# Adding expert rows into the residual in DRAM, and a planned order for the tail

## The chip, the core and the metric

One core of one Trainium2 chip runs the whole kernel. The metric is device microseconds of one launch. The engines are TensorE (PE; PEld is its weight load), VectorE (DVE), ScalarE (ACT), GpSimd (POOL) and SyncE (SP), which only issues transfers here.

## The reference, cut to what matters

One layer of a residual block over 1024 tokens of width 1024. The mixers and the router lie ahead of the change. What follows them is this:

```python
hf = _rmsnorm(x, g_ffn[i]).reshape(B * S, D)
eid, gate = _hier_route(hf, w_group[i], b_group[i], w_expert[i], b_expert[i])
x = x + _routed_experts(hf, eid, gate, w1[i], w3[i], w2[i]).reshape(B, S, D)
e = _rmsnorm(p[i] @ w_ple[i], g_ple_proj[i])
pg = jax.nn.sigmoid(_rmsnorm(x, g_ple[i]) @ w_ple_gate[i])
x = x + pg * e
return _rmsnorm(x, g_final)
```

`_rmsnorm(x, g)` is `x * rsqrt(mean(x*x) + EPS) * g`. Each token goes to 2 of 32 experts of hidden width 512; an expert computes `(silu(xb @ w1) * (xb @ w3)) @ w2`, times the token's gate. `p` has 256 columns.

## The kernel before, in words

Tokens lie in 8 tiles of 128. Products in full precision are made of three matmuls: each operand is split into a high part (`split_hi`, a ScalarE copy, L235) and a low part (`split_lo`, L238, a subtraction on VectorE or GpSimd), and high by high, high by low and low by high are summed in PSUM (`mmr`, L244).

The first stage (mixers, output projection, router) is written as generators whose steps a planner, `Flow` (L63), puts in an order: `go` is an operation with an assumed duration, `get` and `put` count buffers, `on` and `mark` are dependences, `fork` starts another generator. Rank decides between operations that could start within 0.25 us of each other, the lower first. The order in which the planner releases the generators is the order of the instructions on each engine's queue; each engine runs its queue in that order. `c_mix` stores the residual after the mixers to `x2_d` and its norm to `hf_d`, both in DRAM. `c_route` and `tables` (L1099) sum, with one-hot matmuls into `stab`, four columns per expert and slot: the token, the destination row, and two parts of the gate. `fill` (L943) builds their right-hand sides.

The expert loop (L1538) goes over 192 units; an expert has four units for `w1` and `w3` (`up`) and two for `w2` (`down`), and the units of neighbouring experts are interleaved. A unit's two tiles of 512 KB are loaded 13 units ahead (`AHEAD`) and split 2 units ahead (`SL`). Tokens are gathered from `hf_d` by GpSimd (`gather`, L1348), transposed and split. `out_rows` (L1524) scales an expert's output by the gate (`ys`) and scatters its rows (`scatter`, L1353) to `y_d`, which has a row for each token and choice; consecutive scatters are declared independent. The last expert's SiLU, transposes and split (`act_T`) run one behind the other ahead of its `down` units.

The tail is in an order written out by hand (L1567 to L1705). `p` (tiles 4 to 7) and `w_ple` are split, `ple(i)` makes `p @ w_ple` for tiles 5 to 7 in PSUM, squares it for the norm and multiplies by `gp`; tiles 0 to 4 were made in the first stage and are loaded from `e_d` (`e_load`). The gate weights are loaded (`load_wg`, three of them after `last_ys`, three after the first load of `y_d`) and split, five of eight on GpSimd (`WGP`). For each tile `post_load` reads `x2_d`, `load_y` reads the two rows of each token from `y_d` and waits for all scatters, `post_norm` adds them (L1630), squares, and multiplies by the norm factor and `gpl` (L1637) before the transposes; `post_mm` makes the gate product `pg`, 48 matmuls of 512 columns a tile; `post_out` applies the sigmoid, multiplies, adds, norms and stores. The last tile's product is made in two halves of 512 columns.

## Time and profile before

| | us |
|---|---|
| median of 3 runs | 1086.72 (1086.24 to 1089.61) |
| profiled execution, its own time | 1087.43 |
| span of its trace, first to last instruction | 1085.7 |
| mean granted TensorE clock | 0.984 |

The busy time of an engine is the time in which its instructions ran; a matmul's row lasts longer than the step to the next one, since matmuls are pipelined. The granted clock is a share of full speed: 1.00 is 2.4 GHz, 0.50 is 1.2 GHz. The share of the transfers is the mean over 16 transfer engines; where packets overlap it goes above 1. "Idle before" names what ended an engine's wait.

### The profile page before, as it was taken

How to read it: one execution, taken by the hardware profiler on the slowest of the kernel's cores; microseconds unless marked ns; L12 is line 12 of the kernel's file. 1: busy time of each engine (PE TensorE's matmuls, PEld its weight loads, DVE VectorE, ACT ScalarE, POOL GpSimd, SP SyncE). 2: the span in 40 equal slices, each digit the busy share in tenths (PEclk: the TensorE clock that was granted, in tenths of full speed). 3: DMA queues.
4: the chain of work that ended last, by engine and by line, in shares of the span. 5: the costliest groups of instructions: out<-in, count | busy, mean ns of one | idle time of the engine just before them, and what ended most of it. 6: DMA issues, size and time to landing. Idle time of an engine off the chain costs nothing. (4 is left out here: it accounts for less than half of the span.)

```text
span 1085.7 us, 14177 instructions
## 1 busy us (share of the span) xinstructions
PE 1021.4 (94%) x4839; PEld 838.6 (77%) x4840; DVE 931.0 (86%) x1109; ACT 727.3 (67%) x932; POOL 281.9 (26%) x235
## 2 busy tenths in 40 slices
PE   4999999979999799999999999999999999867995
PEld 4887768758888688888888888888888888655884
DVE  5999999999556699999999999999999999669863
ACT  5447878772333688888888888888787888643331
POOL 6459576631210210111111111111010100033110
PEclk9999999999999899999999999999999999979998
DMA  9310002243326889999999999999999999477511
GB/s 270 99 39 20 19 20 78 96 155 118 117 97 207 311 315 405 400 403 401 381 395 391 381 402 385 388 392 385 382 385 382 385 379 394 154 275 290 174 40 58
DMA packets 101070, 281.49 MB, mean 259 GB/s; under 512 B 16849, under 2 KB 34945, under 8 KB 100993
## 3 DMA queue, kind: packets, MB, share of 16 engines
q1 hardware_dynamic: 89216, 255.79, 63.2%
q0 software_dynamic: 10592, 21.01, 5.2%
q10 hardware_dynamic: 1184, 3.75, 0.9%
q8 instruction: 39, 0.64, 0.2%
q14 instruction: 39, 0.31, 0.1%
HBM read 265.28 MB, written 31.98 MB: 274 GB/s over the span
## 5 line engine op out<-in xcount | busy, mean ns | idle before, releaser
L1349 POOL DMA_INDIRECT xg<-hf_d,toki x32 | 43.8, 1370 | 361.0 <-PE xgT L295 348.6
L549 DVE SCALAR_TENSOR_TENSOR fir<-u,V,fir 128x512 f32<-128x512 f32 (+20 forms) x180 | 133.2, 743 | 5.0
L235 ACT ACTIVATE xTh<-xgT 128x512 fp32r<-128x512 f32 x80 | 47.1, 598 | 77.3 <-PE xgT L295 77.3
L584 POOL TENSOR_TENSOR acc<-fpr,acc 128x512 f32<-128x512 f32 x60 | 86.2, 1437 | 40.6 <-ACT fpr L574 37.6
L1354 POOL DMA_INDIRECT y_d<-ys,dsti x32 | 39.1, 1220 | 147.9 <-ACT ys L1526 147.9
L287 POOL TENSOR_TENSOR rs<-ms,mhalf 128x1 f32<-128x1 f32 x32 | 23.2, 727 | 155.2 <-DVE ms L281 155.2
L238 DVE TENSOR_TENSOR xTl<-xgT,xTh 128x512 fp32r<-128x512 f32 x80 | 54.4, 686 | 6.8 <-ACT xTh L235 6.8
L244 PE MATMUL zvg<-hTh,whi 128*128 128x512 f32 (+1 forms) x144 | 56.7, 394 | 0.0
L244 PE MATMUL zvg<-hTh,wlo 128*128 128x512 f32 (+1 forms) x144 | 53.2, 369 | 0.0
L244 PE MATMUL zvg<-hTl,whi 128*128 128x512 f32 (+1 forms) x144 | 53.0, 368 | 0.0
L574 ACT ACTIVATE fpr<-u,V 128x512 f32<-128x512 f32 x60 | 41.9, 717 | 15.4 <-POOL acc L584 15.3
L295 PE MATMUL xgT<-ident,xg 128*128 128x128 f32 x256 | 38.8, 276 | 7.0 <-DVEq L1423 7.0
L295 PEld LDWEIGHTS xgT<-ident,xg 128*128 128x128 f32 x256 | 32.2, 142 | 14.9 <-issue 7.1
L1526 ACT ACTIVATE ys<-ey,gat 128x1024 f32<-128x1024 f32 x32 | 35.4, 1107 | 7.1 <-PE ey L244 7.1
L244 PE MATMUL wo<-wohi,lnyhl 128*128 128x512 f32 x128 | 39.4, 404 | 0.7 <-DVE lnyhl L238 0.7
L238 POOL TENSOR_TENSOR wlo<-wraw,whi 128x1024 fp32r<-128x1024 f32 x14 | 34.3, 2453 | 20.2 <-ACT whi L235 20.2
L1383 ACT ACTIVATE silu<-eab 128x512 f32<-128x512 f32 x32 | 19.2, 599 | 29.0 <-PE eab L244 29.0
L855 ACT ACTIVATE hf<-xre 128x1024 f32<-128x1024 f32 x8 | 8.5, 1058 | 42.0 <-DVE xre L843 33.4
L244 PE MATMUL pg<-wglo,xTh 128*128 128x512 f32 x96 | 32.0, 401 | 3.6 <-POOL wglo L238 2.3
L244 PE MATMUL pg<-wghi,xTl 128*128 128x512 f32 x96 | 31.7, 398 | 1.5 <-DVE xTl L238 1.5
L244 PE MATMUL pg<-wghi,xTh 128*128 128x512 f32 x96 | 32.4, 404 | 0.2 <-ACT xTh L235 0.2
L244 PEld LDWEIGHTS zvg<-hTl,whi 128*128 128x128 f32 x144 | 27.7, 192 | 5.8 <-issue 1.7
(3324 smaller groups left out, 3514.3 us busy)
## 6 DMA issues: line engine op xcount, KB each, us to landing
wraw<-in_w_in_dram SPq DMA_DIRECT2D x16, 512.0 KB, 5.1
yy<-y_d SPq DMA_DIRECT2D x16, 512.0 KB, 5.1
xin<-in_x_dram SPq DMA_DIRECT2D x8, 512.0 KB, 7.1
woraw<-in_w_out_dram SPq DMA_DIRECT2D x8, 512.0 KB, 3.7
xre<-in_x_dram SPq DMA_DIRECT2D x8, 512.0 KB, 4.1
hf_d<-hf POOLq DMA_DIRECT2D x8, 512.0 KB, 5.2
x2r<-x_d SPq DMA_DIRECT2D x8, 512.0 KB, 8.0
wgraw<-in_w_ple_gate_dram SPq DMA_DIRECT2D x8, 512.0 KB, 6.1
```

The lines of the kernel that those rows point to most:

```text
L235: act.activation(r_(hi), src, AF.Copy)
L238: (eng or dve).tensor_tensor(out=r_(lo), in0=src, in1=hi, op=ALU.subtract)
L244: pe.matmul(out=o, lhsT=r_(l), rhs=r_(r), start=start, stop=stop)
L287: pool.tensor_tensor(out=rs, in0=ms, in1=mhalf[:, 0:1], op=ALU.pow)
L295: pe.transpose(out=t[:, k * P:(k + 1) * P], in_=src[:, off + k * P:off + (k + 1) * P], identity=ident)
L549: dve.scalar_tensor_tensor(f[:, a0 - t0:512], u[c][:, a0 - s:t1 - s], tap(c, s), f[:, a0 - t0:512], op0=ALU.mult, op1=ALU.add)
L574: act.activation(pr, u[c][:, 512 - s:1024 - s], AF.Copy, scale=tap(c, s))
L584: pool.tensor_tensor(out=a[:, 512:1024], in0=fprs.pop((c, s)), in1=a[:, 512:1024], op=ALU.add)
L1349: return pool.indirect_dma_start(out=dst, out_offset=None, in_=hf_d, in_offset=bass.IndirectOffsetOnAxis(ap=idx, axis=0), bounds_check=S - ...
L1354: return pool.indirect_dma_start(out=y_d, out_offset=bass.IndirectOffsetOnAxis(ap=idx, axis=0), in_=src, in_offset=None, bounds_check=2 * ...
L1383: act.activation(s_, w[:, 0:512], AF.Silu)
L1526: i = act.activation(ys, yw.pop(e), AF.Copy, scale=gat[:, e:e + 1])
```

## The change

- `scatter` adds the rows of an expert to `x2_d` in the transfer itself (`compute_op`), with the token as the row. `y_d`, the destination column of the tables and the declared independence of the scatters go.
- The tail reads `x2_d` alone. `g_ple` is multiplied into `w_ple_gate` where that is split (`c_wg`), all low parts on VectorE. The raw residual is transposed; its norm factor is the scale of the sigmoid.
- The loads and splits of `p` and `w_ple` and the loads of the gate weights come into the expert loop (`past` counts the units since the last weight load).
- The last two units and the whole tail are ordered by a second planner run. The last expert's output is scaled in two halves, one on ScalarE and one on VectorE. The first tile of `x2_d` is loaded in two halves. The last gate product is made in cuts of 512, 256 and 256 columns, and the last tile is scaled and stored in two halves by two engines.

```diff
+             ("lru_b_r", 4), ("lru_b_i", 4), ("lru_lambda", 4), ("lru_conv_w", 16), ("g_ffn", 8), ("g_ple", 8)]
...
-    gv = [cst.tile([P, NT, 4], F32, name="gv%d" % k) for k in range(2)]
+    gv = [cst.tile([P, NT, 3], F32, name="gv%d" % k) for k in range(2)]
     for k in range(2):
-        for t in range(2):
-            pool.iota(gv[k][:, :, t], pattern=[[P, 8]], base=1 + S * k * t, channel_multiplier=1,
-                      allow_small_or_imprecise_dtypes=True)
+        pool.iota(gv[k][:, :, 0], pattern=[[P, 8]], base=1, channel_multiplier=1, allow_small_or_imprecise_dtypes=True)
...
         dve.tensor_scalar(tok, T[:, 0:NE], -1.0, None, op0=ALU.add)
-        dve.tensor_scalar(dst, T[:, NE:2 * NE], -1.0, None, op0=ALU.add)
-        dve.tensor_copy(gat, T[:, 2 * NE:3 * NE])
-        dve.tensor_tensor(out=gat, in0=gat, in1=T[:, 3 * NE:4 * NE], op=ALU.add)
+        dve.tensor_copy(gat, T[:, NE:2 * NE])
+        dve.tensor_tensor(out=gat, in0=gat, in1=T[:, 2 * NE:3 * NE], op=ALU.add)
 
...
     def scatter(src, idx):
-        return pool.indirect_dma_start(out=y_d, out_offset=bass.IndirectOffsetOnAxis(ap=idx, axis=0),
-                                       in_=src, in_offset=None, bounds_check=2 * S - 1, oob_is_err=False)
+        return pool.indirect_dma_start(out=x2_d, out_offset=bass.IndirectOffsetOnAxis(ap=idx, axis=0),
+                                       in_=src, in_offset=None, bounds_check=S - 1, oob_is_err=False,
+                                       compute_op=ALU.add)
 
...
     def out_rows(e):
         ys = m4("ys")
-        i = act.activation(ys, yw.pop(e), AF.Copy, scale=gat[:, e:e + 1])
-        sc = scatter(ys, dsti[:, e:e + 1])
-        if scs:
-            tc.declare_no_dep(sc.ins, scs[-1].ins, reason="every row has one writer")
-        scs.append(sc)
-        return i
+        act.activation(ys, yw.pop(e), AF.Copy, scale=gat[:, e:e + 1])
+        scatter(ys, toki[:, e:e + 1])
+
+    wgr = {}
+    pl = {}, {}, {}
+
+    def load_wg(k):
+        wgr[k] = slot("wgraw")
+        load(wgr[k], A["w_ple_gate"][0][rows(k), :])
 
...
+    for s, (e, g) in enumerate(units[:-2]):
+        past = s + AHEAD - len(units)
+        if past == 0:
+            pt = p_load(1)
+        elif past == 1:
+            pw = {k: wp_load(k) for k in range(2)}
+        elif past > 2 and len(wgr) < 8:
+            load_wg(len(wgr))
+        load_unit(s + AHEAD)
...
+        if past in (5, 6):
+            k = past - 5
...
+            pl[0][1, k], pl[1][1, k] = o[:, 0:512], o[:, 512:1024]
+        elif past in (7, 8):
+            k = past - 7
+            hi, lo = slot("wphi"), slot("wplo")
+            split_hi(hi, pw[k])
+            split_lo(lo, pw[k], hi)
+            pl[2][k] = hi, lo
+    fl = Flow({"s": NSLOT - 24, "m4": NM, "m2": 4, "wp": 1, "yp": 1, "tp": 2, "a": 4}, OFF2)
+    fl.table = "silu"
...
+    def c_last():
+        e = NE - 1
+        yield get("m2")
+        yield go("ACT", 0.75, set="silu")
+        w = abw.pop(e)
+        s_ = m2("silu")
+        act.activation(s_, w[:, 0:512], AF.Silu)
+        yield go("DVE", 0.69)
+        dve.tensor_tensor(out=s_, in0=w[:, 512:1024], in1=s_, op=ALU.mult)
+        yield put("wp")
+        yield get("tp")
+        yield go("PE", 0.45, lag=0.35)
+        t = act_tr(s_)
+        yield put("m2")
+        yield get("m2", 2)
+        hi, lo = m2("hhi"), m2("hlo")
+        yield go("ACT", 0.6)
+        split_hi(hi, t)
+        yield go("DVE", 0.69)
+        split_lo(lo, t, hi)
+        yield put("tp")
+        yield get("yp")
+        w = None
+        for j in range(4):
+            yield go("PE", 6 * MM, lag=0.35 if j == 3 else 0.0)
+            w = w or ytile()
+            y_mm(w, (hi, lo), j, his[len(units) - 2 + j // 2][j % 2])
+            if j == 3:
+                yield put("m2", 2)
+            yield put("s", 2)
+        yield get("m4")
+        ys = m4("ys")
+        yield ("fork", -90, c_half(w, ys))
+        yield go("ACT", 0.6)
+        act.activation(ys[:, 0:512], w[:, 0:512], AF.Copy, scale=gat[:, e:e + 1])
+        yield on("ys1")
+        yield put("yp")
+        yield go("POOL", 1.1, lag=4.5)
+        scatter(ys, toki[:, e:e + 1])
+        yield put("m4")
+        yield mark("sc")
+
+    def c_half(w, ys):
+        yield go("DVE", 0.69)
+        dve.tensor_scalar(ys[:, 512:1024], w[:, 512:1024], gat[:, NE - 1:NE], None, op0=ALU.mult)
+        yield mark("ys1")
+
...
+    def c_ple2(i):
+        yield get("wp")
+        w = None
+        for k in range(2):
+            for si in range(3):
+                yield go("PE", 2 * MM, lag=0.35 if k and si == 2 else 0.0)
+                w = w or wtile("ple")
+                ple_mm(w, i, pl, [(k, si)])
+        yield get("s")
+        es_[i] = slot("er")
+        yield ("fork", -1, c_esq(i, w))
+        yield on("gp")
+        yield go("DVE", 1.22)
+        dve.tensor_tensor(out=es_[i], in0=w, in1=gpb, op=ALU.mult)
+        yield on(("eq", i))
+        yield put("wp")
+        yield mark(("e", i))
+
...
+    def c_wg(k):
+        yield get("s", 2)
+        yield go("ACT", 1.05)
         hi, lo = slot("wghi"), slot("wglo")
...
+        act.activation(r_(hi), wgr[k], AF.Copy, scale=vec("g_ple", k))
+        yield go("DVE", 1.22, port=True)
+        dve.scalar_tensor_tensor(r_(lo), wgr[k], vec("g_ple", k), hi, op0=ALU.mult, op1=ALU.subtract)
+        yield put("s")
+        wgs[k] = (hi, lo)
+        yield mark(("wg", k))
+
+    def c_x2(i):
+        yield on("sc")
+        if i >= 2:
+            yield on(("xT", i - 2, 1))
+        yield get("s")
         xs[i] = slot("x2r")
...
+        if i == 0:
+            yield ("fork", -59.5, c_xh())
+        yield go("SP", 0.7 if i == 0 else 1.35, lag=2.6)
+        cs = slice(0, 512 if i == 0 else D)
+        load(xs[i][:, cs], x2_d[rows(i), cs])
+        yield mark(("xl", i))
+        if i == 0:
+            yield on("xh")
+        yield mark(("x", i))
+
+    def c_xh():
+        yield go("SP", 0.7, lag=2.6)
+        load(xs[0][:, 512:D], x2_d[rows(0), 512:D])
+        yield mark("xh")
+
+    def c_xt(i):
+        yield on(("xl", i))
+        if i:
+            yield on(("xt", i - 1))
+        yield get("a", 2)
+        xT[i] = aslot("xTh"), aslot("xTl")
+        for q in range(2):
+            yield on(("x" if q else "xl", i))
+            yield get("tp")
+            yield go("PE", 0.45, lag=0.35)
+            t = ttile("x2T")
+            transposes(t, xs[i], off=q * 512)
+            yield ("fork", -40, c_xs(i, q, t))
+        yield mark(("xt", i))
+
+    def c_xs(i, q, t):
+        qs = slice(q * 512, (q + 1) * 512)
+        yield go("ACT", 0.6)
+        split_hi(xT[i][0][:, qs], t)
+        yield go("DVE", 0.69)
+        split_lo(xT[i][1][:, qs], t, xT[i][0][:, qs])
+        yield put("tp")
+        yield mark(("xT", i, q))
+
...
+    def c_pg(i, n):
+        last = i == NT - 1
+        cuts = ((0, 512), (512, 768), (768, 1024)) if last else ((0, 1024),)
+        if i:
+            yield on(("pgd", i - 1))
+        yield get(psum(n))
+        w = None
+        ss = sm("ss5", 3) if last else sm("ss5")
+        for c, (a, b) in enumerate(cuts):
             for k in range(8):
...
+                yield on(("xT", i, k // 4))
+                yield on(("wg", k))
+                yield go("PE", 6 * MM * (b - a) / 1024, lag=0.35 if k == 7 else 0.0)
+                w = w or ptile(n)
+                hi, lo = wgs[k]
                 ks = slice(k * P, (k + 1) * P)
...
+                xh, xl = xT[i]
+                for si, (l_, rr) in enumerate(((xh[:, ks], hi), (xh[:, ks], lo), (xl[:, ks], hi))):
+                    for o in range(a, b, 512):
+                        e = min(o + 512, b)
+                        mmr(w[:, o:e], l_, rr[:, o:e], k == 0 and si == 0, k == 7 and si == 2)
+            if c == len(cuts) - 1:
+                yield mark(("pgd", i))
+                yield put("a", 2)
+            yield ("fork", 20 + i, c_out(i, n, c, len(cuts), a, b, w, ss))
+
+    def c_out(i, n, c, nc_, a, b, w, ss):
+        f = (b - a) / 1024
+        cs = slice(a, b)
+        yield on(("rsx", i))
+        yield on(("e", i))
+        if c == 0:
+            yield get("m4")
+            sgs[i] = m4("sgp")
+        sg, xt, e = sgs[i], xs[i], es_[i]
+        yield go("ACT", 0.17 + 0.9 * f, set="sig")
+        act.activation(sg[:, cs], w[:, cs], AF.Sigmoid, scale=rsx[:, i:i + 1])
+        if c == nc_ - 1:
+            yield put(psum(n))
+        yield go("DVE", 0.14 + 1.08 * f, port=True)
+        dve.scalar_tensor_tensor(sg[:, cs], sg[:, cs], rse[:, i:i + 1], e[:, cs], op0=ALU.mult, op1=ALU.mult)
+        yield go("DVE", 0.14 + 1.08 * f, port=True)
+        dve.tensor_tensor(out=xt[:, cs], in0=xt[:, cs], in1=sg[:, cs], op=ALU.add)
+        yield go("ACT", 0.36 + 0.9 * f)
+        act.activation(sg[:, cs], xt[:, cs], AF.Square, accum_out=ss[:, c:c + 1])
+        yield mark(("sq", i, c))
+        if nc_ > 1:
+            yield on("gfin")
+            yield go("DVE", 0.14 + 1.08 * f, port=True)
+            dve.tensor_tensor(out=xt[:, cs], in0=xt[:, cs], in1=gfin[:, cs], op=ALU.mult)
+            yield mark(("xf", c))
+        if c < nc_ - 1:
+            return
+        for k in range(nc_):
+            yield on(("sq", i, k))
+        yield put("s")
+        yield put("m4")
+        if nc_ > 1:
+            yield go("DVE", 0.2)
+            s1 = sm("ss6")
+            dve.tensor_reduce(s1, ss, op=ALU.add, axis=AX.X)
+            ss = s1
+        yield go("DVE", 0.15)
+        ms = ms_of(ss, D)
+        yield go("POOL", 0.55)
+        rs = rs_of(ms)
+        if nc_ > 1:
+            yield ("fork", -1, c_end(xt, rs))
+            yield go("DVE", 0.4)
+            dve.tensor_scalar(xt[:, 512:D], xt[:, 512:D], rs, None, op0=ALU.mult)
+            yield go("SP", 0.7, lag=2.6)
+            load(out[0][rows(i), 512:D], xt[:, 512:D])
+            return
+        yield on("gfin")
+        yield go("DVE", 1.22, port=True)
+        dve.scalar_tensor_tensor(xt, xt, rs, gfin, op0=ALU.mult, op1=ALU.mult)
+        yield go("SP", 1.35, lag=2.6)
+        load(out[0][rows(i), :], xt)
+        yield put("s")
+
+    def c_end(xt, rs):
+        yield go("ACT", 0.6)
+        act.activation(xt[:, 0:512], xt[:, 0:512], AF.Copy, scale=rs)
+        act.dma_start(out=out[0][rows(NT - 1), 0:512], in_=xt[:, 0:512])
+
+    fl.add(-90, c_last())
+    fl.add(-99, c_vec(gpb, A["g_ple_proj"], "gp"))
+    for k in range(8):
+        fl.add(RK2["wg"] + k, c_wg(k))
+    for i in range(NPG):
+        fl.add(RK2["e"] + i, c_e(i))
     for i in range(NPG, NT):
...
+        fl.add(RK2["ple"] + i, c_ple2(i))
+    fl.add(-10, c_vec(gfin, A["g_final"].unsqueeze(0), "gfin"))
     for i in range(NT):
...
+        fl.add(-60 + i, c_x2(i))
+        fl.add(-50 + i, c_xt(i))
+        fl.add(RK2["xrs"] + i, c_xrs(i))
+        fl.add(10 + i, c_pg(i, i))
+    fl.add(0, c_free([("e", i) for i in range(NPG, NT)], 6))
+    fl.run()
+    mctx.close()
```

## Rows read from the trace of the kernel before

**Rows 1.** The page, busy time: us, share of the span, instructions.

```profile
PE 1021.4 (94%) x4839; PEld 838.6 (77%) x4840; DVE 931.0 (86%) x1109; ACT 727.3 (67%) x932; POOL 281.9 (26%) x235
```

**Rows 2.** Busy us and instructions by stretch; then granted clock, transfers' share, GB/s.

```profile
500.00:700.00 200.00, 200.00 (x948) 165.28 (x947) 185.38 (x181) 164.25 (x191) 28.82 (x22) 1.00 1.01 390
...
923.00:939.00 16.00, 16.00 (x73) 12.93 (x71) 14.76 (x14) 12.83 (x14) 0.97 (x1) 1.00 0.51 190
...
948.00:960.00 12.00, 9.81 (x36) 7.84 (x36) 3.37 (x5) 4.51 (x7) 1.05 (x2) 0.86 0.63 223
960.00:968.00 8.00, 0.26 (x2) 0.00 (x0) 6.04 (x9) 4.12 (x8) 1.59 (x3) 0.82 1.02 407
968.00:975.00 7.00, 5.72 (x16) 4.24 (x17) 7.00 (x5) 5.59 (x7) 6.75 (x4) 0.50 0.60 229
975.00:993.00 18.00, 12.42 (x53) 8.77 (x51) 15.91 (x14) 7.06 (x10) 11.20 (x5) 0.99 0.73 283
993.00:1074.00 81.00, 80.59 (x380) 67.21 (x380) 57.97 (x67) 27.45 (x46) 9.54 (x13) 1.00 0.33 119
...
988.00:994.00 6.00, 2.85 (x15) 2.03 (x16) 6.00 (x9) 4.54 (x6) 1.40 (x1) 1.00 1.03 419
```

**Rows 3.** The chain that ended last: start us, us, what.

```profile
972.85 2.72 DVE x2r L1630
...
979.31 4.57 DMA x2r<-x_d
...
999.61 0.88 PE xgT L295 x8
...
1055.56 18.84 PE pg L244 x83
```

**Rows 4.** Groups by line and shape, 945 to 1086: busy us, mean ns.

```profile
L1630 DVE TENSOR_TENSOR x2r<-x2r,yy 128x1024 f32<-128x1024 f32 x16 | 22.7, 1416 | 0.1
...
L238 POOL TENSOR_TENSOR wglo<-wgraw,wghi 128x1024 fp32r<-128x1024 f32 x5 | 14.7, 2968 | 0.1
```

**Rows 5.** Timeline of TensorE, 938 to 1000: start us, us, instruction.

```profile
940.45 0.66 PE L295 MATMUL hTp<-ident,silu 128*128 128x128 f32 x4 [1.41 <-DVE silu L1384]
...
946.92 0.62 PE L244 MATMUL ey<-ehi__9264,hlo 128*128 128x512 f32 x2
...
959.64 0.61 PE L244 MATMUL ple<-wphi,phl 128*128 128x512 f32 x2
968.02 1.97 PE L295 MATMUL xgT<-ident,n 128*128 128x128 f32 x8 [7.76 <-DVE ms L281]
```

**Rows 6.** Timeline of all engines around the last scatter.

```profile
948.98 0.97 POOL L1354 DMA_INDIRECT y_d<-ys,dsti  x1 [12.98 <-ACT ys L1526]
...
956.26 0.80 SPq L1622 DMA_DIRECT2D yy<-y_d  x2
```

**Rows 7.** Timeline of ScalarE at the start.

```profile
4.40 1.06 ACT L311 ACTIVATE xn<-xin 128x1024 f32<-128x1024 f32 x1 [0.96 <-DMA xin<-in_x_dram]
```

**Rows 8.** The tile ys: ns min/median/max, first and last start us.

```profile
L1526 ACT ACTIVATE ys<-ey,gat x32: 1102/1107/1121, 402.1 to 947.6; 128x1024 f32<-128x1024 f32 x32
L1354 POOL DMA_INDIRECT y_d<-ys,dsti x32: 972/1239/1247, 403.5 to 949.0; - x32
...
DMA to landing us min/median/max: 7.0/7.6/8.7
```

**Rows 9.** The tile sgp: ns min/median/max, by shape at the end.

```profile
L1664 DVE SCALAR_TENSOR_TENSOR sgp<-sgp,rse,er x9: 746/1276/1286, 995.1 to 1075.1; 128x1024 f32<-128x1024 f32 x7, 128x512 f32<-128x512 f32 x2
```

**Rows 10.** The output in DRAM: issue to landing of its nine stores.

```profile
DMA to landing us min/median/max: 2.0/2.6/3.1
```

**Rows 11.** Timeline of TensorE, two matmuls of 256 columns in sequence.

```profile
24.43 0.28 PE L244 MATMUL zvg<-hTl,whi 128*128 128x256 f32 x1
24.55 0.28 PE L244 MATMUL zvg<-hTh,wlo 128*128 128x256 f32 x1
```

**Rows 12.** Timeline of VectorE at the end of the kernel.

```profile
1078.39 1.41 DVE L1672 SCALAR_TENSOR_TENSOR x2r<-x2r,rs,gfin 128x512 f32<-128x512 f32 x2 [0.73 <-POOL rs L287]
```

More of the change, by code (lines that the diff above doesn't have):

```diff
@@ L35 @@
 NA = 5
-GM = 1
 HS = 5
@@ L39 @@
 EARLY = (3, 4, 5, 6, 7, 8, 9)
-PN0 = 6
 NPG = 5
-WGP = (1, 2, 3, 4, 5)
-PLU = 0
-PLW = 0
-WG0 = 2
-WG1 = 5
+OFF2 = {}
+RK2 = {"pT": -30, "wp": -29, "wg": 0, "e": 12, "ple": -5, "xrs": 2}
 WDVE = (8, 11)
@@ new lines, in _body @@
+    rsx = cst.tile([P, NT], F32, name="rsx")
+    def c_last():
[39 more added lines that the diff above has]
+        yield mark("sc")
@@ L1615, in post_load @@
-    def post_load(i):
-        xs[i] = slot("x2r")
-        load(xs[i], x2_d[rows(i), :])
-    def load_y(i):
-        for k in range(2):
-            yys[i, k] = m4("yy")
-            q = nc.sync.dma_start(out=yys[i, k], in_=y_d[k * S + i * P:k * S + (i + 1) * P, :])
-            for sc in scs:
-                order(q, sc, True)
-        return q
-    def post_norm(i):
-        xt = xs[i]
-        for k in range(2):
-            a = dve.tensor_tensor(out=xt, in0=xt, in1=yys.pop((i, k)), op=ALU.add)
-            if k == 0:
-                order(a, ei[PN0 if i == 0 else NT - 1])
-        ss = sm("ss4")
-        n3 = m4("n3")
-        act.activation(n3, xt, AF.Square, accum_out=ss)
-        rs = rstd_of(ss, D)
-        dve.scalar_tensor_tensor(n3, xt, rs, gpl, op0=ALU.mult, op1=ALU.mult)
-        xTp[i] = gather_T(n3)
@@ L1675, in _body @@
-    post_load(0)
-    for k in range(WG0):
-        load_wg(k)
-    load(gpl, A["g_ple"].broadcast_to([P, D]))
-    for k in range(WG0, WG1):
-        order(load_wg(k), last_ys, True)
-    y0 = load_y(0)
-    for k in range(WG1, 8):
-        order(load_wg(k), y0)
-    post_load(1)
-    load_y(1)
-    gfin = slot("gfin")
-    load(gfin, A["g_final"].unsqueeze(0).broadcast_to([P, D]))
-    for i in range(NPG, NT):
-        ple(i)
-        if i == PN0:
-            post_norm(0)
-    for i in range(8):
-        split_wg(i)
```

205 lines of the change are left out of this document (79 added, 126 removed).

## The prediction

> **What bounds the kernel now.** I began with the page. TensorE is busy 1021.4 of 1085.7 us [rows 1], so a gain has to come from its gaps or from the work after its last matmul. The busy time by stage says where the gaps are [rows 2]. While the experts run, from 500 to 700, TensorE is busy 200 of 200 us, VectorE 185.4, ScalarE 164.3, and the transfers move 390 GB/s. From 993 to 1074 TensorE is full again, and nothing else is near its limit. Between them lies the poor stretch: 9.8 of 12 us busy from 948 to 960, 0.3 of 8 to 968, 5.7 of 7 to 975 at a granted clock of 0.50 (the 1.2 GHz level), 12.4 of 18 to 993. That is 16.8 us without a matmul, and more than 3 us of half speed.
>
> The chain of waits names what stands there [rows 3]: adding the two expert rows to the residual on VectorE (L1630, 2.72 us in one piece of the chain), a reload of the residual (4.57 us), transposes. The groups of this stretch by shape give the volume [rows 4]: 16 adds of 22.7 us in all, and five splits of the gate weights on GpSimd that take 14.7 us, 2.97 each. So the tail waits behind four things in a row: the last scatter, reading both expert rows back, adding and normalising on VectorE, and splitting weights late.
>
> The last scatter and the work around it are in the timeline [rows 5, 6]. The last expert's output matmuls end at about 947.4, its scatter is issued at 948.98, and the first read of its rows at 956.26, when it has landed: 7.3 us. TensorE ends the three `ple` products at about 960.2 (959.64 and one piece) and transposes nothing until 968.02.
>
> **The change part by part.** I follow one chain, from the last expert to the end, on the clock of the profiled execution (1087.43 us, span 1085.7).
>
> *Start and routing.* One small load more on ScalarE's queue (`g_ple`): an issue takes 0.40 us on SP (two in 0.80 [rows 6]), and ScalarE waits 0.96 us for `x` there [rows 7], which hides it. `fill` writes 96 columns a tile instead of 128 and `tables` has one operation less. I take -0.3 us for these; between -0.5 and +0.5.
>
> *Scatter with add, experts 0 to 30.* Experts are 17.6 us apart (31 steps from 402.1 to 947.6), a scatter lands in 7.6 us [rows 8]. Consecutive scatters now wait for each other, since the declaration that they are independent is gone; that wait ends some 10 us before the next one is issued, and the gathers queued behind it on GpSimd lose nothing. What is not seen in this trace is an adding transfer. Below, it costs nothing beyond a plain one. Nearest above: it reads the destination too. An expert has 2048/32 = 64 rows of 4 KB, 0.262 MB; at 419 GB/s, the rate of the stretch from 988 to 994, in which the transfers never stood [rows 2], that is 0.63 us per expert. The stage moves 390 GB/s where 419 are to be had, so the transfers have 17.6 x (1 - 390/419) = 1.2 us to spare per expert. Cost taken: 0. The cover is this 1.2 us; if it is gone, every microsecond above it costs 31.
>
> A rule bears on this: the Trainium skill, "Collectives: The Full Stack", section "The bandwidth ceiling", holds that an add in the transfer engine costs no cycles of its own but a second source read, on the same ring as the first. By it the adding scatter takes the 0.63 us above and the stage stays TensorE's; no run so far shows it here.
>
> *Work moved into the expert loop.* Two groups of four transposes of `p`, with their splits, and the split of `w_ple` come into units 184 to 187. TensorE gets eight transposes, 0.88 us at full clock [rows 3]: +0.9. VectorE gets two splits of 512 and two of 1024 columns, some 3.6 us, where it has 14.8 of 16 us busy from 923 to 939 [rows 2], 1.2 us free. Splits run two units (near 6 us) ahead of their matmuls, so the rest is taken from that lead; cost 0, at most 2.
>
> *Last expert.* Its SiLU, transposes and split leave TensorE a hole (1.41 us of it before the transposes [rows 5]) which the plan fills with `ple` pieces of 0.45 us. The planner counts the low part's split before it releases the output matmuls, so I expect about three pieces too many in front of them: +1.4 (0 to 2). Scaling the output as two halves on two engines takes 0.75 us (the half pass of [rows 9]) for 1.11 [rows 8] and saves 0.4. The scatter is issued at 948.98 - 0.3 + 0.9 + 1.4 - 0.4 = 950.6.
>
> *Its landing.* 7.3 us for the plain one. Lower end: no difference. Upper end: a second trip as long as the first, 14.6. The data of one scatter are little and the way is mostly latency, so I stay near the plain row and add 1.5 us for reading first: 959.4.
>
> *To the first gate matmul.* No rows to add, no norm: the half tile of `x2_d` is issued (0.3) and lands (2.6 us, the median of the output stores [rows 10]; 2.0 to 4.6, the reload in the chain [rows 3]). Four transposes at the low clock take 1.0 (eight took 1.97 [rows 5]); ScalarE's high half 0.6. First gate matmul: 963.9. By then the gate weights are split: their loads are issued from unit 182 on, and ScalarE and VectorE have over 20 us from the end of the expert loop for eight passes each of at most 1.28 us [rows 9]. The five GpSimd splits become VectorE's; the cover is the wait for the scatter, and without it they would cost up to 6 us.
>
> *Gate products.* 360 matmuls of 512 columns at 0.227 us, the pitch of the last piece of the chain (83 in 18.84 us [rows 3]), 81.6 us; the last half tile in two cuts of 256, 48 at 0.12 [rows 11], 5.8; 60 transposes left at 0.11 (eight in 0.88 [rows 3]), 6.6. TensorE will have idled from about 954 to 962; before, after an idle of 7.8 us, it worked 7 us at the 0.50 clock [rows 2, 5]. I charge the same: half of 7.4, 3.7. Sum 97.7, end at 1061.6. A tile takes TensorE 48 x 0.227 + 8 x 0.11 = 11.8 us; VectorE needs two half passes and four whole ones for it, 6.6 us by [rows 9], ScalarE no more, and the `x2` and `e` loads of 0.5 MB each come where the transfers run at a third of their rate [rows 2]. So the plan has room. The norm factor as the sigmoid's scale and `g_ple` in the weights take a VectorE pass of 1.28 us per tile out of the path into TensorE; that is how the 963.9 comes about, and is not counted again.
>
> *End.* The last matmul ends at 1074.4 [rows 3], 0.2 us after its slot; from the slot to the end of the span there are 11.5 us. Four steps shrink from 512 to 256 columns: 0.746 against 1.276 us for twice the width [rows 9] gives about 0.25 each, 1.0. The two closing multiplications, 1.41 us one behind the other [rows 12], run side by side in 0.7. One small reduction stays as it was. 11.5 - 1.6 = 9.9 us: 1071.5.
>
> The span falls by 14.2 us, the profiled 1087.43 to 1073.2. The median of the runs, 1086.72, stands 0.7 lower, so **1072.5 us**.
>
> **The rivals.**
> *The transfers become the bound (slower).* If an adding row costs much more than one extra read, the expert stage goes to the speed of the transfers. Price: per expert, what the adds cost beyond 1.2 us, 31 times. The gain of 14.2 us is gone at 0.46 us beyond, 1.7 us of extra transfer time per scatter, 2.7 plain reads of its rows. At four reads, 2.5 us, it is 31 x 1.3 = 40 us: 1112.8 us. For it: 390 of 419 GB/s is close. Against: 1.7 us is much for 0.262 MB that a plain transfer moves in 0.63. Chance 0.10.
>
> *The wait is only moved.* The adding scatter lands in 14.6 us, and with nothing left for TensorE to do the whole 5.8 us more show: 1078.3. For it: the landing is mostly fixed latency, and a read before the write may double it. Chance 0.13.
>
> *The planned tail starves TensorE.* Order on four in-order queues is fixed from estimated times; if a slot or an engine is late by 1.8 us for each of eight tiles, the gain is gone: 1087. Against: VectorE at half load, ScalarE below. Chance 0.06.
>
> *Better than forecast.* The hole holds just the pieces that fit, the add costs no landing time, the clock stays up: 1.4 + 1.5 + 3.7 less, 1065.9. Against: the same idle of 8 us did lower the clock. Chance 0.11.
>
> *It does not do what it says*: some wait for the whole residual in DRAM could hold the first loads back until much later than the last scatter; that has the look and the price of the third rival and is counted there.
>
> **How the numbers follow.** 0.60 is left for the forecast. Its own terms reach from -5 (no added landing, no surplus pieces, and half the clock's charge) to +7 (2 us of late splits, 3 us of stalls in the tail, 2 us of slower loading). The range takes in the good case and the moved wait: 1065 to 1081, leaving out the first and third rivals and a little of the rest. A measurement can tell 0.3%, 3.3 us, from no change. Faster by more: forecast, moved wait, better case, 0.84, of which 0.01 is taken off for a tail that loses part of its gain: 0.83. Slower by more: the first rival (0.10) and a sliver of the third, 0.11. Between: 0.06.
>
> **What would show it.** Right: expert spacing still 17.6 us and TensorE still 200 of 200 from 500 to 700, at some 400 GB/s; the last scatter issued near 950.6 and read from near 959.4; the first gate matmul near 964, and TensorE without gaps from about 970 to 1062; under 10 us after it. Wrong: TensorE waiting for expert weights and a spacing above 17.8 us; a last scatter of over 11 us; idle TensorE between gate tiles; an unlowered clock near 965.

## The result, and the profile after

The changed kernel is **slower**: 1115.99 us in the median of 4 runs (1114.17 to 1117.82) against 1087.26 us for the kernel before, ratio 1.026, 95% interval 1.024 to 1.028. I had forecast 1072.5, so 43.5 us are to be explained.

The page of the changed kernel, its busy time and the head of its chain of waits:

```profile
span 1116.1 us, 14187 instructions
...
PE 1034.1 (93%) x4863; PEld 840.4 (75%) x4864; DVE 901.2 (81%) x1094; ACT 740.4 (66%) x936; POOL 295.5 (26%) x228
...
DMA 37%; PE 26%; DVE 3%; ACT 2%; issue 2%; SPq 0%; POOLq 0%; ACTq 0%; DVEq 0%
```

TensorE has the same work as before [rows 1], but the chain that ended last now runs over transfers for 37% of the span. The stretches say where (columns as in [rows 2]):

```profile
500.00:700.00 200.00, 194.42 (x900) 155.85 (x899) 176.22 (x173) 161.46 (x184) 35.34 (x21) 1.00 0.99 366
700.00:900.00 200.00, 194.74 (x898) 155.60 (x897) 174.09 (x171) 159.72 (x182) 36.73 (x21) 1.00 0.99 364
940.00:960.00 20.00, 10.10 (x47) 8.16 (x45) 10.39 (x10) 8.67 (x10) 1.59 (x1) 0.84 1.00 374
...
994.00:1000.00 6.00, 1.65 (x8) 1.03 (x6) 4.96 (x6) 1.32 (x4) 4.39 (x3) 0.83 0.20 27
1000.00:1010.00 10.00, 5.16 (x17) 4.00 (x18) 3.15 (x5) 2.83 (x5) 0.00 (x0) 0.50 0.85 307
1010.00:1074.00 64.00, 64.00 (x301) 52.97 (x300) 29.66 (x41) 24.09 (x38) 6.80 (x11) 0.99 0.26 92
```

From 500 to 700 TensorE does 900 matmuls where it did 948 [rows 2], and the transfers, busy throughout, move 366 GB/s and not 390: the expert stage has become theirs. ScalarE's splits wait here for loads of weights, up to 2.7 us at a time; in the kernel before they never did from 500 to 900. (The 366 counts no second read by the add: the profile has 256.37 MB read from HBM here and in e9_free below, which leaves the add out. Counted once per expert, 0.262 MB would make it 380.) Ahead of the tail, from 940 to 960, TensorE works 10.1 of 20 us. From 1010 on it is full, as forecast. The tile `ys` of the changed kernel (ns min/median/max, first and last start):

```profile
L1343 POOL DMA_INDIRECT x_d<-ys,toki x32: 1574/1962/5932, 404.6 to 994.3; - x32
L1512 ACT ACTIVATE ys<-ey,gat x31: 1096/1102/1112, 403.2 to 976.6; 128x1024 f32<-128x1024 f32 x31
...
DMA to landing us min/median/max: 5.9/9.3/11.0
```

The first `ys` comes 1.1 us later than before, and the scatter lands in 9.3 us and not 7.6 [rows 8]. The last of these 31 stands behind a wait that happens once, shown below; so I take the spacing from the second expert to the thirtieth, 28 steps, in every run. The same tile in that stretch, kernel before and changed kernel:

```profile
L1526 ACT ACTIVATE ys<-ey,gat x29: 1102/1107/1112, 419.8 to 917.4; 128x1024 f32<-128x1024 f32 x29
```

```profile
L1512 ACT ACTIVATE ys<-ey,gat x29: 1096/1102/1112, 420.9 to 942.4; 128x1024 f32<-128x1024 f32 x29
```

The experts lie (942.4 - 420.9)/28 = 18.62 us apart, where before it was 17.77. The timeline of TensorE (waits in brackets) has the second loss and the tail:

```profile
949.50 0.60 PE L288 MATMUL hTp<-ident,silu 128*128 128x128 f32 x4
964.32 1.09 PE L1158 MATMUL pT<-ident,p_in 128*128 128x128 f32 x4 [14.21 <-DMA p_in<-in_p_dram]
...
983.19 0.66 PE L288 MATMUL hTp<-ident,silu 128*128 128x128 f32 x4 [0.99 <-DVE silu L1586]
...
986.88 0.62 PE L238 MATMUL ey<-ehi__9265,hhi 128*128 128x512 f32 x2
...
1002.88 1.12 PE L288 MATMUL x2T<-ident,x2r 128*128 128x128 f32 x4 [7.23 <-DMA x2r<-x_d]
...
1007.07 1.09 PE L288 MATMUL x2T<-ident,x2r 128*128 128x128 f32 x4 [1.79 <-DMA x2r<-x_d]
1007.80 1.20 PE L238 MATMUL pg<-wghi,xTh 128*128 128x512 f32 x2
```

TensorE's queue stood 14.2 us at the transposes of `p`, with ready matmuls of the last two experts behind them. Why the load was late is in the timeline of SP:

```profile
949.03 0.33 SPq L235 DMA_DIRECT2D eraw__8956<-in_w_dram  x1
952.70 0.33 SPq L235 DMA_DIRECT2D eraw__8958<-in_w_dram  x1
953.95 0.39 SPq L235 DMA_DIRECT2D p_in<-in_p_dram  x1
```

`p_in` stands behind all expert weights in SP's queue, which the transfers now hold back. From the last scatter, at 994.27, to the end take 121.8 us, where before it was 1085.7 - 948.98 = 136.7 and my forecast had 1071.5 - 950.6 = 120.9. The tail gained nearly what it should; the last scatter goes out 45.3 us later than before and 43.7 later than forecast.

### The profile page after: what moved, and what is told of

It reads as the page before. It is cut to its first block, busy times and chain, and to the rows that moved or that the text cites. A ratio compares the mean times of both kernels' runs of the same rounds, so it can differ in the third digit from the quotient of the medians.

```text
span 1116.1 us, 14187 instructions
## 1 busy us (share of the span) xinstructions
PE 1034.1 (93%) x4863; PEld 840.4 (75%) x4864; DVE 901.2 (81%) x1094; ACT 740.4 (66%) x936; POOL 295.5 (26%) x228
## 3 DMA queue, kind: packets, MB, share of 16 engines
HBM read 256.37 MB, written 31.98 MB: 258 GB/s over the span
## 4 chain that ended last, share of the span: by engine, by line
DMA 37%; PE 26%; DVE 3%; ACT 2%; issue 2%; SPq 0%; POOLq 0%; ACTq 0%; DVEq 0%
PE ey L238 8%; PE eab L238 7%; PE pg L238 6%; PE ple L238 2%; DMA eraw__4845<-in_w_dram 1%; DMA eraw__7573<-in_w_dram 1%; DMA eraw__8121<-in_w_dram 1%; DMA eraw__4152<-in_w_dram 1%; DMA eraw__6176<-in_w_dram 1%; DMA eraw__5630<-in_w_dram 1%; DMA eraw__4538<-in_w_dram 1%; DMA eraw__8360<-in_w_dram 1%; DMA eraw__7450<-in_w_dram 1%; DMA eraw__6722<-in_w_dram 1%; DMA eraw__4661<-in_w_dram 1%
## 5 line engine op out<-in xcount | busy, mean ns | idle before, releaser
L1338 POOL DMA_INDIRECT xg<-hf_d,toki x32 | 48.7, 1521 | 352.2 <-PE xgT L288 339.8
L1343 POOL DMA_INDIRECT x_d<-ys,toki x32 | 64.8, 2026 | 168.6 <-ACT ys L1512 161.2
L229 ACT ACTIVATE xTh<-xgT 128x512 fp32r<-128x512 f32 x64 | 37.6, 589 | 13.6 <-PE xgT L288 13.0
L232 DVE TENSOR_TENSOR xTl<-xgT,xTh 128x512 fp32r<-128x512 f32 x64 | 43.6, 684 | 0.5 <-ACT xTh L229 0.5
L1790 DVE SCALAR_TENSOR_TENSOR sgp<-sgp,rse,er 128x1024 f32<-128x1024 f32 (+2 forms) x10 | 10.7, 1071 | 37.0 <-ACT sgp L1786 37.0
L280 POOL TENSOR_TENSOR rs<-ms,mhalf 128x1 f32<-128x1 f32 x24 | 14.2, 593 | 93.9 <-DVE ms L274 93.8
L238 PE MATMUL pg<-wghi,xTh 128*128 128x512 f32 (+1 forms) x104 | 34.1, 391 | 1.4 <-ACT sgp L1786 1.4
L1512 ACT ACTIVATE ys<-ey,gat 128x1024 f32<-128x1024 f32 x31 | 34.2, 1102 | 0.0
L238 PE MATMUL pg<-wglo,xTh 128*128 128x512 f32 (+1 forms) x104 | 32.8, 378 | 0.0
L238 PE MATMUL pg<-wghi,xTl 128*128 128x512 f32 (+1 forms) x104 | 32.8, 378 | 0.0
```

The lines of the kernel that those rows point to most:

```text
L229: act.activation(r_(hi), src, AF.Copy)
L232: (eng or dve).tensor_tensor(out=r_(lo), in0=src, in1=hi, op=ALU.subtract)
L238: pe.matmul(out=o, lhsT=r_(l), rhs=r_(r), start=start, stop=stop)
L280: pool.tensor_tensor(out=rs, in0=ms, in1=mhalf[:, 0:1], op=ALU.pow)
L1338: return pool.indirect_dma_start(out=dst, out_offset=None, in_=hf_d, in_offset=bass.IndirectOffsetOnAxis(ap=idx, axis=0), bounds_check=S - ...
L1343: return pool.indirect_dma_start(out=x2_d, out_offset=bass.IndirectOffsetOnAxis(ap=idx, axis=0), in_=src, in_offset=None, bounds_check=S - ...
```

## The experiments

**1. The changed kernel without the add, and with `p` later.** The first leaves the add out (rows overwrite); the second moves two steps by three and two units.

```diff
 e1_plain
-            in_=src, in_offset=None, bounds_check=S - 1, oob_is_err=False,
-            compute_op=ALU.add)
+            in_=src, in_offset=None, bounds_check=S - 1, oob_is_err=False)
 e2_later
-        if past in (5, 6):
+        if past in (8, 9):
-        elif past in (7, 8):
+        if past in (9, 10):
```

> The changed kernel with plain scatters into the residual, the add left out (so the expert rows replace the residual rows instead of being added); every wait between scatters stays. Theory A (the second read of an adding transfer costs the expert stage): spacing of the experts from 500 to 900 back from 18.9 to 17.7 us, transfers back to some 390 GB/s, time near 1080 to 1090. Rival C (the scatters' waits for each other, or the residual as destination, cost the time): spacing stays at 18.9, time stays near 1116.

> The changed kernel with the transposes of p three units later and the splits of w_ple two units later in the expert loop. Theory (TensorE's queue stood 14.2 us behind a transpose of p whose load had not landed): the wait is gone, time near 1102, and the expert spacing stays at 18.9. Rival (the last experts' weights would have been late by as much): under 4 us gained, 1112 or more.

Measured: 1082.65 us and 1107.96 us, one run each. The tile `ys` of e1_plain, then of e2_later, from the second expert to the thirtieth:

```profile
L1511 ACT ACTIVATE ys<-ey,gat x29: 1103/1105/1115, 421.4 to 918.7; 128x1024 f32<-128x1024 f32 x29
```

```profile
L1512 ACT ACTIVATE ys<-ey,gat x29: 1095/1100/1112, 420.2 to 939.4; 128x1024 f32<-128x1024 f32 x29
```

Without the add the spacing is (918.7 - 421.4)/28 = 17.76 us, that of the kernel before, although the scatters still wait for each other and go to the residual: rival C falls. With the add it is 18.54. e2_later made the wait at `p` shorter and did not end it:

```profile
961.24 1.12 PE L1158 MATMUL pT<-ident,p_in 128*128 128x128 f32 x4 [5.72 <-DMA p_in<-in_p_dram]
```

So its theory (no wait, near 1102) and its rival (under 4 us gained) both missed. There are two losses, and the add is the larger: 33.3 us between the changed kernel and e1_plain, against 8.0 for moving `p`.

**2. Are the scatter's rows dealt unevenly to the transfer engines?** The slots of an expert were spread over all partitions; e4_both has the later `p` as well.

```diff
+    pool.iota(slots.rearrange("p (a b) -> p a b", a=16), pattern=[[1, 16], [16, 8]], base=0,
+              channel_multiplier=0, allow_small_or_imprecise_dtypes=True)
...
-                dve.tensor_scalar(r_(R), iot, ranks[k][:, i:i + 1], None, op0=ALU.is_equal)
+                dve.tensor_scalar(r_(R), slots, ranks[k][:, i:i + 1], None, op0=ALU.is_equal)
```

> The changed kernel with the token slots of an expert spread over the partitions (rank r at partition 8*(r mod 16) + r div 16 instead of r), so that some 64 rows lie on all 128 partitions and not on the first half. Theory A (the mean transfer time is used up by the second read): no change, spacing 18.9, near 1116. Theory B (each block of partitions belongs to one transfer engine; rows on half of them load half of the engines, and a weight load ends with the slowest): spacing back to 17.7 or 17.8, near 1080 to 1090.

> The changed kernel with both: spread slots, and the transposes of p and splits of w_ple later. Theory A: only the second counts, near 1102, spacing 18.9. Theory B: spacing 17.7 and no wait for p, near 1072 to 1076, faster than both kernels.

Measured: 1111.45 us (one run), and 1106.1 us (ratio to before 1.016, 1.014 to 1.018). The tile `ys` of e3_spread:

```profile
L1515 ACT ACTIVATE ys<-ey,gat x29: 1095/1100/1112, 421.1 to 936.9; 128x1024 f32<-128x1024 f32 x29
```

18.42 us apart instead of 18.62; in e4_both 18.47 instead of e2_later's 18.54. The spreading is worth 0.1 to 0.2 us an expert, and Theory B, which expected 17.7, falls as the main cause.

**3. The planned tail with plain scatters.** Each token's two rows go to `y_d` again and VectorE adds them in the tail; all else is the changed kernel with the later `p`.

```diff
+    y_d = dr.tile([2 * S, D], F32, name="y_d")
...
-        return pool.indirect_dma_start(out=x2_d,
-            compute_op=ALU.add)
+        return pool.indirect_dma_start(out=y_d,
...
+                dve.tensor_tensor(out=xs[i][:, a:b], in0=xs[i][:, a:b], in1=yy[k][:, a:b], op=ALU.add)
```

> The planned tail and the rest of the change, with the work of p three units later, but the expert rows scattered plainly to a row of their own as before, and added on VectorE in the tail (first tile in halves, the two reads in tiles that the gathers no longer use). If the adds in the transfers were the only loss of the expert stage and the tail is worth its forecast: spacing 17.7 us, and 1076 to 1080, faster than both kernels. If the tail's gain came from having no rows to add: 1085 or more.

Measured: 1086.95 us, ratio 0.9994 (0.9985 to 1.0003), the same as before. Timelines of this run around its last expert, VectorE and then GpSimd:

```profile
939.06 1.22 DVE L232 TENSOR_TENSOR wplo<-wpraw,wphi 128x1024 fp32r<-128x1024 f32 x1
...
942.46 1.22 DVE L232 TENSOR_TENSOR wplo<-wpraw,wphi 128x1024 fp32r<-128x1024 f32 x1
943.60 0.68 DVE L1600 TENSOR_TENSOR silu<-eab,silu 128x512 f32<-128x512 f32 x1
944.20 2.47 DVE L1701 SCALAR_TENSOR_TENSOR wglo<-wgraw,V,wghi 128x1024 fp32r<-128x1024 f32 x2
946.59 0.69 DVE L232 TENSOR_TENSOR hlo<-hTp,hhi 128x512 fp32r<-128x512 f32 x1
...
956.02 0.75 DVE L1636 TENSOR_SCALAR ys<-ey,gat 128x512 f32<-128x512 f32 x1 [1.56 <-ACT ys L1626]
```

```profile
957.06 1.01 POOL L1348 DMA_INDIRECT y_d<-ys,dsti  x1 [7.87 <-DVE ys L1636]
```

The tail is short, 1084.9 - 957.06 = 127.8 us against 136.7. But the last scatter comes 8.1 us later than before [rows 6], and that takes nearly all of the gain of 8.9. The product with SiLU stands behind splits of `w_ple` in VectorE's queue, the split of h behind two splits of the gate weights, and the second half of `ys` begins when the first has ended: two halves in series, not side by side. This was a third loss, hidden under the other two.

**4. The price of a transfer in the expert stage.** e2_later with more transfers for each expert but the last, 64 rows each: the same rows added to a second copy (e6), scattered plainly to it (e7), stored in one piece (e10), loaded in one piece (e11).

```diff
 e6_add_twice
+        pool.indirect_dma_start(out=z_d, out_offset=bass.IndirectOffsetOnAxis(ap=toki[:, e:e + 1], axis=0),
+                                in_=ys, in_offset=None, bounds_check=S - 1, oob_is_err=False,
+                                compute_op=ALU.add)
 e7_add_and_plain
+        pool.indirect_dma_start(out=z_d, out_offset=bass.IndirectOffsetOnAxis(ap=toki[:, e:e + 1], axis=0),
+                                in_=ys, in_offset=None, bounds_check=S - 1, oob_is_err=False)
 e10_store
+        nc.scalar.dma_start(out=z_d[e * 64:(e + 1) * 64, :], in_=ys[0:64, :])
 e11_load
+        nc.scalar.dma_start(out=zt, in_=hf_d[(e % 16) * 64:(e % 16) * 64 + 64, 0:1008])
```

> As e2_later, with every expert's rows (but the last's) also added to a second copy of the residual, so the suspected cost is there twice and the stage is bound by transfers throughout. If an adding scatter costs the time of its packets, two reads of 64 rows over 16 engines, 1.3 us: spacing 20.0 against 18.7, 1147. If it holds up the other transfers beyond that: 21 or more, 1180.

> As e2_later, with every expert's rows (but the last's) also scattered plainly to a second copy of the residual. By its packets a plain scatter costs 0.63 us once the stage is bound by transfers: spacing 19.3, 1127. The difference to the run that adds twice is what the add costs over a plain scatter under that bound.

> e2_later with one more transfer for each expert but the last: 64 rows of ys, as many as an expert has on average, stored in one piece to a table that nothing reads, on ScalarE's queue. It asks why a further plain scatter cost 1.27 us per expert (e7_add_and_plain against e2_later, 39.4 us over 31) and a further adding one 2.61 us, about twice what their packets take on 16 engines (64 times 159 or 327 ns over 16, so 0.64 and 1.31). Theory one, any write in this stage costs about twice its packets: the store costs 1.2 to 1.3 us per expert too, and the run takes 1145 to 1149 us. Theory two, the indirect form on GpSimd's queue costs the other half: the store costs 0.5 to 0.8 us per expert, and the run takes 1123 to 1133 us.

> e2_later with one more load for each expert but the last: 64 rows of the normalised activations, 4032 bytes of each, in one piece to a tile that nothing reads, on ScalarE's queue. Theory one of e10_store in its stricter form, that a write costs more than a read: this run takes 1123 to 1130 us (0.5 to 0.7 us per expert, by the 366 GB/s of the stage 0.70) while e10_store takes 1145 or more. Rival, every byte that is added to this stage costs alike, whichever way it goes: e10_store and this run lie within 6 us of each other.

Measured: 1188.99, 1147.36, 1142.27 and 1150.94 us, one run each of e6 and e7 and two each of e10 and e11. The times hold waits that happen once: the one at `p`, and in e10 and e11 one in the first step between experts, where ScalarE stands with its first further transfer next in its queue, 15.7 us in e10 and 16.1 in e11 (why was not settled). Here e10:

```profile
419.38 0.51 ACTq L1515 DMA_DIRECT2D z_d<-ys  x1
419.94 1.06 ACT L229 ACTIVATE ehi__3837<-eraw__3217 128x1024 fp32r<-128x1024 f32 x1 [15.68 <-DMA eraw__3715<-in_w_dram]
```

So the price per expert is read from the spacing, second expert to thirtieth, which leaves these out; here e6, e7, e10, e11 in this order:

```profile
L1515 ACT ACTIVATE ys<-ey,gat x29: 1095/1099/1102, 423.5 to 1015.5; 128x1024 f32<-128x1024 f32 x29
```

```profile
L1515 ACT ACTIVATE ys<-ey,gat x29: 1094/1099/1111, 423.6 to 977.4; 128x1024 f32<-128x1024 f32 x29
```

```profile
L1513 ACT ACTIVATE ys<-ey,gat x29: 1098/1104/1115, 436.4 to 977.2; 128x1024 f32<-128x1024 f32 x29
```

```profile
L1512 ACT ACTIVATE ys<-ey,gat x29: 1100/1105/1111, 437.0 to 986.4; 128x1024 f32<-128x1024 f32 x29
```

| one more per expert | spacing us | more than e2_later's 18.54 |
|---|---|---|
| stored in one piece | 19.31 | 0.77 |
| loaded in one piece | 19.62 | 1.08 |
| plain scatter | 19.78 | 1.24 |
| adding scatter | 21.14 | 2.60 |

Single steps vary by more than a microsecond (17.7 to 21.5 in e10), so the second digit is not sure. e6 did what its second case says (21 or more, 1180), and e7's 0.63 us by packets missed. In e10 neither time came, with the wait of 15.7 us in it; by the spacing its second theory fits, with the store at 0.77 us and as many rows in the indirect form at 1.24. In e11 the load costs 1.08 and so no less than the store, against its theory; its rival (all alike, within 6 us) missed too, with 8.7. A further 0.26 MB in this full stage costs 0.8 to 1.2 us, where 0.72 would be its part at the stage's 366 GB/s. And the adding scatter costs 2.60 - 1.24 = 1.36 us more than the plain one, so the add alone costs as much as another transfer of the same rows, or a little more.

**5. The order round the last expert mended, and the add free.** e8_order is e5_plain_y with the order changed as below, where "hl" marks the last expert's split of h and "yd" its weighted rows: the splits of `w_ple` (`c_wp`) come behind the one, the `ple` products and six of the gate weights' splits behind the other. e12_order2 moves the second transposes of `p` (`c_p`) behind "hl" as well, and the products with the stored rows behind the first tile's adds. e9_free is e2_later with the add left out.

```diff
 e8_order
-        if past in (9, 10):
...
+    def c_wp(k):
+        yield on("hl")
...
-        act.activation(ys[:, 0:512], w[:, 0:512], AF.Copy, scale=gat[:, e:e + 1])
...
-        dve.tensor_scalar(ys[:, 512:1024], w[:, 512:1024], gat[:, NE - 1:NE], None, op0=ALU.mult)
+        act.activation(ys, w, AF.Copy, scale=gat[:, e:e + 1])
+        yield mark("yd")
...
     def c_ple2(i):
+        yield on("yd")
...
     def c_wg(k):
+        yield on("hl" if k < 2 else "yd")
 e12_order2
+    def c_p():
+        yield on("hl")
...
     def c_e(i):
         yield on("sc")
+        yield on(("x", 0))
```

> This is e5_plain_y (planned tail, plain scatter to y_d, rows added on VectorE in the tail) with three edits to the order round the last expert: the two splits of w_ple come behind the last expert's h split and not in units 187 and 188, the weighted rows of the last expert are made by one instruction and not by two halves, and all of the splits of w_ple_gate but two, and the pieces of p times w_ple, come behind those rows. Theory: in e5_plain_y VectorE's queue held the last expert back, 2.4 us of w_ple splits ahead of the product with silu (939.06 and 942.46), two splits of w_ple_gate ahead of the h split, and the second half of the rows waited for the first (955.30 and 956.02), so that the scatter was issued at 957.06, 8.1 us behind the kernel before. It should now be issued at 950 to 953, and the run take 1080 to 1084 us, 0.3 to 0.6% under the kernel before. Rival: the splits of w_ple_gate, eight times 1.28 us on VectorE, and the adds of the rows now stand together ahead of the first gate product, which comes at 970 or later as in e5_plain_y (972.2), and the run takes 1085 to 1088 us, the same as the kernel before.

> This is e2_later (the transposes of p three units later) with the scatters plain and not adding; what is left out is the add, so the rows overwrite. Theory: the adds in the bound stage cost some 0.9 us per expert and the transposes of p behind their late load 6 us of their own without any adds, so this run has no wait ahead of the transposes of p over 1 us, experts 17.7 to 17.8 us apart, and takes 1075 to 1079 us; against e2_later that makes 29 to 33 us for the adds alone. Rival: the stall of p in e1_plain was filled afterwards by slack and cost nothing, and the run takes 1081 to 1084 us as e1_plain did.

> e8_order with two more edits: the second transposes of p with their split come behind the last expert's h split, and the products of the stored rows of p times w_ple come behind the adds of the first tile. Theory: in e8_order VectorE's queue still stood ahead of the last expert by one split (938.50, 0.68 us) and ahead of the first tile's adds by three products with the stored or new rows (964.48 to 967.94); without them the adds start at 964.5 to 966.5 and not at 967.94, and the run takes 1080 to 1083 us. Rival: the loads of the scattered rows land no sooner than that, the adds start at 967 or later all the same, and the run takes 1083.5 to 1086 us as e8_order did.

Measured: e8_order 1084.63 us, ratio 0.9961 (0.9947 to 0.9976); e12_order2 1084.12 us, 0.9954 (0.9938 to 0.9970); e9_free 1078.47 us, 0.9912 (0.9895 to 0.9929). In e8_order the scatter goes out at

```profile
953.44 0.97 POOL L1348 DMA_INDIRECT y_d<-ys,dsti  x1 [15.80 <-ACT ys L1618]
```

which is 3.6 us earlier than in e5_plain_y, and 2.3 us of it reach the end. The time lies between those of the theory and its rival, and both have a part, for the first gate product came at 971.50 and not much before 972.18. TensorE, left without `ple` products, ran the last expert's first output matmuls at the low clock (0.66 granted from 940 to 950). In e12_order2 that product came at 969.44, and the time is not distinguishable from e8_order's. Its adds began at 965.88, as its theory had it, and its time is the rival's. Both are faster than the kernel before by some 0.4%, without an adding transfer. e9_free has a spacing of (917.9 - 420.6)/28 = 17.76 us and no wait ahead of the transposes of `p`:

```profile
L1511 ACT ACTIVATE ys<-ey,gat x29: 1103/1105/1116, 420.6 to 917.9; 128x1024 f32<-128x1024 f32 x29
```

## Why the prediction was wrong

The 43.5 us are the sum of three steps, each with its own run (e2_later a single one): 1072.5 + 6.0 = 1078.5 (e9_free), + 29.5 = 1108.0 (e2_later), + 8.0 = 1116.0.

**Scatter with add, cost 0 taken: 29.5 us, the step that failed.** "the transfers have 17.6 x (1 - 390/419) = 1.2 us to spare per expert" and the extra read "is 0.63 us" were both off, by the same mistake: I priced a small transfer at the rate of the best stretch. In the stage it costs 0.8 to 1.2 us, and the add 1.36. Against e9_free, whose TensorE is full, the adds lengthen the spacing by 18.54 - 17.76 = 0.78 us; as they cost 1.36, there was about 0.6 us to spare and not 1.2. In 28 steps that is 21.8 us. Another 6.3 lie in the step behind them, 24.4 us against 18.1, in which e2_later still waits for `p`, and 2.6 in the landing of the last scatter (5.79 us against 3.18): 30.7 in all, where the two traces' spans differ by 30.4. The trace of before held the means to see it. Its weights come in twelve loads of 0.524 MB per expert, and SP's timeline of that kernel shows how fast one follows another when nothing intervenes:

```profile
612.46 0.33 SPq L241 DMA_DIRECT2D eraw__5820<-in_w_dram  x1
613.71 0.33 SPq L241 DMA_DIRECT2D eraw__5822<-in_w_dram  x1
614.95 0.33 SPq L241 DMA_DIRECT2D eraw__5849<-in_w_dram  x1
```

At (614.95 - 612.46)/2 = 1.245 us each, twelve take 14.9 us; of the 17.77 us of an expert, 2.8 are left, for a gather and a scatter that, by the prices measured since for a load and a plain scatter, cost 1.08 + 1.24. That makes 0.5 us spare, a working after the fact, near the 0.6. A gap of 29 GB/s between two average rates does not show such a bound, and the same row of [rows 2] has the transfers' share at 1.01, so it shows no idle time either. My 17.6 us was also a mean over 31 steps of which the last two are short (16.2 and 14.0 us); the stage's own spacing is 17.77, so my mark of 17.8 stood almost on the kernel before.

The Trainium skill, "Collectives: The Full Stack", section "The bandwidth ceiling", says that an add in the transfer costs no cycles of its own but a second source read. The price fits: 1.36 us more than a plain scatter, 1.08 for a load of nearly the same bytes. That the add is a read, the runs do not show, for the count of bytes read is the same with and without it (256.37 MB). The 0.63 us was my price and not the rule's.

My first rival named this mechanism and gave 1112.8 us, at a chance of 0.10. That it lies near the outcome is half chance: its price of 2.5 us less its slack of 1.2 is 1.3 us per expert where 0.78 came, and the other losses make up the rest. I held 1.7 us per scatter to be the point from which it decides; with the slack as measured it is 0.46 + 0.6, about 1.1, and the add's 1.36 is past it.

**Work moved into the expert loop, "VectorE ... cost 0, at most 2": 8.0 us for `p`, some 6 more within the 29.5, and some 4 of the next step.** I counted VectorE's free time and TensorE's transposes, and not when the data arrive. The load of `p` is issued behind the last weights and lands in 10.2 us, so its transposes stood in front of TensorE's in-order queue. Without any add the same place costs 1082.65 - 1078.47 = 4.2 us, so the step would have been wrong even with a free add.

**Last expert, scatter forecast at 950.6: 5.6 us of the remaining 6.0.** (The rest nearly cancels: e9_free takes 1075.9 - 956.17 = 119.7 us from the scatter to the end where I had 120.9, and its profiled execution lies 0.9 under its median where I had put it 0.7 over.) In e9_free it is issued at

```profile
956.17 1.01 POOL L1343 DMA_INDIRECT x_d<-ys,toki  x1 [7.45 <-DVE ys L1621]
```

Its transposes of h come at 945.08 where my terms gave 940.45 - 0.3 + 0.9 = 941.05: that is the work moved into the loop, whose 3.6 us on VectorE I had set to 0 because a lead would take them up. The last expert has no lead to draw on: its product with SiLU starts at 944.34, when the second split of `w_ple` (943.20) has ended. The remaining 1.5 us lie behind it: TensorE starts the output matmuls 3.7 us behind these transposes and not 1.3 as before, so the surplus pieces cost 2.4 and not 1.4, and the halves of `ys`, counted as -0.4, ran in series and took 0.69 + 0.75 us.

**Its landing and the way to the first gate product, 13.3 us forecast: 13.5, by two errors that cancel.** The adding scatter landed in 5.95 us in the chain, so the 7.3 + 1.5 was 2.9 us too high; but the plan put the transposes of the second tile ahead of the first gate product, and they waited for their own load until 1007.07.

```profile
994.27 5.95 DMA x_d<-ys,toki
...
1001.19 5.74 DMA x2r<-x_d
...
1007.07 1.09 PE x2T L288 x4
...
1102.50 2.78 PE pg L238 x21
```

The landing was wrong in both its parts. I took the 7.3 us of the plain scatter from a place where three loads of gate weights were issued beside it (that these made the difference was not tested); in e9_free, at the place it has in the changed kernel, a plain scatter lands in 3.18. These are the kernel before, then e9_free's chain:

```profile
948.73 1.28 SPq L241 DMA_DIRECT2D wgraw<-in_w_ple_gate_dram  x3
```

```profile
956.17 3.18 DMA x_d<-ys,toki
```

So the add took 2.8 us at the landing and not 1.5. The moved wait (second rival) did not occur, at 5.95 us against its 14.6, but its reason was near: with the add the landing takes nearly twice the plain one's time.

**Gate products, 97.7 us: right in the sum.** From 1007.80 to 1105.28 they take 97.5 us. The granted clock of 0.50 from 1000 to 1010 was in it; but from 1007.80 on it lasts only to about 1012, which is some 2 us by half of that time (an estimate) and not 3.7, and 1.4 us go to waits for ScalarE at the last cuts that I did not have. **End, 9.9 us:** 1116.1 - 1105.28 = 10.8, so 0.9 short. **Start, -0.3:** +1.1 by the first `ys`. ScalarE's first norm begins 0.28 us later (4.68 against 4.40), so the further load on its queue did not hide; the rest was not isolated, and the runs with the same first stage lie between +0.4 (e2_later) and +3.7 (e7_add_and_plain).

The mark I set, a spacing above 17.8 us with TensorE waiting for weights, was the one that came, though TensorE's own waits from 500 to 900 (10.6 us) are for splits and products of h, which stand in ScalarE's and VectorE's queues behind splits that wait for weights. What failed in the odds was holding "390 of 419 GB/s is close" to be weak evidence at 0.10.

## What to carry to other kernels

In a stage where TensorE and the transfers are both near full, price a further transfer by the pitch at which whole loads follow each other and by what a like transfer adds there, not by a difference of average rates. Work moved into a loop with free time on average is not free at the loop's last turn, where it stands in front of the one chain that everything after waits for; and a step put into an in-order queue needs the landing time of its data, not only its issue. When several losses overlap, undoing one at a time may show a further one beneath, and the size of each depends on what else is undone (the add 33.3 or 29.5 us, the place of `p` 8.0 or 4.2). And a price per step is read from the steps themselves: a total, or a mean that takes in the first or the last of them, can hold a wait that happens once.

## What was not expected of the hardware

- A transfer of 0.26 MB in the expert stage costs 0.77 us as a store, 1.08 as a load and 1.24 as a plain scatter, where weights come at 0.524 MB in 1.25 us. The transfers' share stayed at 0.97 to 1.00 in these three runs from 500 to 900. Why the margin is dearer than the mean was not settled.
- The scatter's queue of the changed kernel took more of the transfer engines for the same bytes; the page's rows, first of the kernel before, then of the changed one:

```profile
q0 software_dynamic: 10592, 21.01, 5.2%
```

```profile
q0 software_dynamic: 10592, 21.02, 7.0%
```

 7.0% of 1116.1 less 5.2% of 1085.7 is 21.7 us, 0.68 per scatter. In the traces' packets from 500 to 900 a 4 KB packet takes 159 ns in the median, and those of the adding scatter 327; (327 - 159) x 64 / 16 gives the same 0.67 us. So of the 1.36 us that an add costs, only half shows as time of its own packets.
- With the transfers otherwise idle, the plain scatter of the last expert lands in 3.18 us (e9_free) and the adding one in 5.95, 5.79 in e2_later. In the full stage the medians are 7.6 and 9.3.
